# Paged attention over the cache in a hybrid decoder step: values read one slot later, sigmoids and buffers of the weight chain rearranged

## The chip, the cores and the metric

The kernel runs on one core of a Trainium2 chip, in float32. The metric is the device time of one execution in microseconds (us); lower is better. Below, PE is TensorE (matmuls), DVE is VectorE, ACT is ScalarE, POOL is GpSimd and SP is SyncE. Here POOL issues the gathers of cache pages and SP the other transfers.

## What is computed

A two-layer decoder step over 528 prompt positions and 64 sample positions (8 sequences of 8 tokens). Each layer is a feed-forward block, a mixer and a second feed-forward block. The mixer has an SSD part (a state-space scan) and a stick-breaking attention part with 8 heads of 64. The change touches the attention of the sample tokens to their past: 2048 cached positions per sequence, in 16 pages of 128.

```python
def sb_block(q, start, k, v, key_valid, bias):
    z = jnp.einsum('bqhd,bkhd->bhqk', q, k).astype(jnp.float32) * (SB_HEAD_DIM ** -0.5)
    z = z + bias.astype(jnp.float32)[None, :, None, None]
    ...
    log_stay = jnp.where(allowed, jax.nn.log_sigmoid(-z), 0.0)
    log_after = lax.cumsum(log_stay, axis=3, reverse=True) - log_stay
    w = jnp.where(allowed, jnp.exp(jax.nn.log_sigmoid(z) + log_after), 0.0)
    return jnp.einsum('bhqk,bkhd->bqhd', w.astype(v.dtype), v)
...
k_past = cache_k[l][page_table].reshape(db, -1, SB_HEADS, SB_HEAD_DIM)
v_past = cache_v[l][page_table].reshape(db, -1, SB_HEADS, SB_HEAD_DIM)
```

The weight of a key is its own sigmoid times the product of "what stays", sigmoid(-z), over all later keys. The kernel computes it with products instead of logarithms: a reverse running product of sigmoid(-z), shifted by one, times sigmoid(z).

## The kernel before

**Order.** The program is written in the order of `run`: feed-forward, mixer, feed-forward, for each layer. A list scheduler then sets the order of every engine's instructions before the run, by priorities and by its own timing; each engine works its list in order. Inside `mixer` the paged past (`past`) has the priority of its place in the program, and the other parts (convolution, scan, keys, gates, prompt attention, output projection) carry priorities of their own, so their matmuls stand between the slots of the past as filler.

**Slots.** `past` (L1458) works in slots x. In slot x the keys of sequence s = x // 4, part i = x % 4, are handled. Part i gathers two tiles of 128 x 1024 (`key_pages`, POOL, L1508), DVE transposes them in blocks into `kt` (`turned`, L1519), and PE multiplies 32 small matmuls into the PSUM bank `sc` (`scores`). There is one `sc` bank, and a new `sc` tile begins in every second slot. After every second slot ACT turns the bank into `be` = sigmoid(z) and `st` = sigmoid(-z), for two groups of four heads ("quads"): four ACTIVATEs of 128 x 256, in the order be, st, be, st (`sigmoids`, L1292 and L1293).

**The chain from scores to weights.** After a sequence's fourth slot `past_weights` (L1532) runs: DVE scans `st` of each quad (`stay`, L1298), takes the total product of each of four stretches (`tot`, L1537), PE transposes `tot`, DVE multiplies the carries of the later stretches into `car` (L1543 to L1545), PE transposes back, DVE copies `cq` (L1548). Then for each quad: DVE multiplies be x carry x shifted `st` (L1552) and the last column be x carry (L1553), PE transposes the result in four pieces into the one PSUM bank `pw` (L1556), and ACT copies it to the weight tile `wt` (L1558).

**Values.** In slot x the value pages of part vi = (x - 6) % 4 of sequence v = (x - 6) // 4 are also gathered (`value_pages`, L1569) and multiplied with the weights (`weigh`, 16 matmuls into `po`). So two slots lie between a sequence's last scores and its first values. The values of the last sequence follow after the loop. `gathered` collects `po` once per sequence (L1589 to L1594).

**What ties slots together.** `together` makes the first matmul of a slot wait for all that the slot's score and value matmuls read: `kt`, both value pages and both `wt`. Key and value pages share six buffers (tag `kn`). `be` and `st` share a pool of four (tag `pb`), one set, so a sequence's sigmoids take the buffers that the previous sequence's products and transposes free. `wt` has two buffers, one for each quad. `qbd`, the block-diagonal queries of a sequence, is one tile that ACT refills (L1471).

**After the past.** The four column pairs of the first half of the output projection stand behind `last_sc`, `last_pw` and `last_po`, the last score, weight and value matmuls.

Of the kernel before, what the change touches and what calls it, by code (L numbers as in the profile page):

```python
# [8 lines left out]
F32 = mybir.dt.float32  # L9
# [3 lines left out]
AF = mybir.ActivationFunctionType  # L13
ALU = mybir.AluOpType
# [13 lines left out]
def const_arrays():  # L28
    p = np.arange(128)
    f = np.float32  # L30
    a32 = np.arange(32)
    c = {}
    c["ident"] = np.eye(128)
    c["ones"] = np.ones((128, 1))
    c["half"] = p[:, None] // 64 == np.arange(32)[None, :]
    o8 = np.zeros((128, 64))
    q64 = np.arange(64)
    same = q64[:, None] // 8 == q64[None, :] // 8
    o8[:64] = same
    c["one8"] = o8  # L40
    c["srep"] = p[:, None] % 32 == p[None, :] % 32
    a16 = np.arange(16)[None, :]
    c["sel16"] = (p[:, None] % 8 == a16 % 8) & (p[:, None] // 32 % 2 == a16 // 8)
    c["mko"] = ((p[:, None] // 8) % 4 == np.arange(4)[None, :])
    sm = np.zeros((128, 8))
    sm[:64] = q64[:, None] // 8 == np.arange(8)[None, :]
    c["seqm"] = sm
    dsel = np.zeros((128, 8))
    for h in range(8):
        dsel[h, h] = 1.0  # L50
        dsel[32 + h, h] = 1.0
    c["dsel"] = dsel
    c["koff"] = ((p % 8) * 16)[:, None]
    c["voff"] = ((p % 32) * 4)[:, None]
    c["mg"] = p[:, None] // 8 == a16
    c["mx"] = p[:, None] // 32 == np.arange(4)[None, :]
    c["kt16"] = np.broadcast_to(np.arange(16)[None, :], (128, 16))
    return {k: np.ascontiguousarray(v.reshape(128, -1)).astype(f) for k, v in c.items()}
# [48 lines left out]
class Kern:  # L107
# [169 lines left out]
    def setup_rest(self):  # L277
        nc, I = self.nc, self.I
# [39 lines left out]
        for h in range(4):  # L318
            v = self.hp[32 * h:32 * h + 32, 32:48].rearrange("p (x h) -> p x h", h=4)[:, :, h]
# [4 lines left out]
        for m in range(4):  # L324
            v = self.hp[32 * m:32 * m + 32, 32:48].rearrange("p (l m h) -> p l m h", l=2, h=2)[:, :, m, :]
            o = self.bt4[32 * m:32 * m + 32, :].rearrange("p (s l h) -> p s l h", s=2, l=2)
# [24 lines left out]
        for l in range(2):  # L351
# [4 lines left out]
            vi = self.cst([128, 32, 2], f"vi{l}", I32)  # L356
# [11 lines left out]
        self.Cbd = [self.cst([128, 2, 128], f"cbd{i}") for i in range(1)]  # L368
        for t in self.Cbd:
            nc.gpsimd.memset(t, 0.0)  # L370
        self.car = [self.cst([128, 128], f"car{i}") for i in range(2)]
        self.tot = [self.cst([128, 128], f"tot{i}") for i in range(2)]
        for t in self.car + self.tot:
            nc.gpsimd.memset(t, 1.0)

        self.dtw = [self.cst([128, 4, 40], f"dtw{h}", F32R) for h in range(2)]
        for t in self.dtw:
            nc.gpsimd.memset(t.bitcast(F32), 0.0)
        self.zero = self.cst([128, 1], "zero")
        nc.gpsimd.memset(self.zero, 0.0)  # L380

# [1076 lines left out]
    def past(self):  # L1458


        nc, l = self.nc, self.l
        self.oP = self.cp.tile([128, 4, 64], F32, name="oP", tag="oP")
        wts = {}
        late = lambda x: (x // 4, x % 4)
        for x in range(34):
            s, i = late(x)
            v, vi = late(x - 6)
            if s < 8 and i == 0:
                qbd = self.QBD[0]
                for a in range(4):  # L1470
                    nc.scalar.copy(qbd[32 * a:32 * a + 32, :, a, :].rearrange("p (b m) q -> p b m q", b=4),  # L1471
                                   self.rep[32 * a:32 * a + 32, :, :, 8 * s:8 * s + 8])
                be = [self.kv.tile([128, 512], F32, name="pbe", tag="pb", bufs=4) for _ in range(2)]
                st = [self.kv.tile([128, 512], F32, name="pst", tag="pb", bufs=4) for _ in range(2)]
            if s < 8 and i % 2 == 0:
                sc = self.own("sc", [128, 2, 256])
            kns = self.key_pages(s, i) if s < 8 else None
            vs = self.value_pages(v, vi) if v >= 0 else None
            kts = self.turned(kns) if kns else None
            if v >= 0 and vi == 0:  # L1480
                po = self.own("po", [128, 512])
            with self.together():
                if kts:
                    self.scores(sc, i % 2, kts, qbd)
                if vs:
                    self.weigh(po, vi, vs, wts[v])
            if s < 8 and i % 2:
                for quad in range(2):
                    c = 2 * l + quad
                    f = lambda t: t.rearrange("p (i t) -> p i t", t=16)[:, :, 8 * (i // 2):8 * (i // 2) + 8]  # L1490
                    self.sigmoids(f(be[quad]), f(st[quad]), sc[:, quad].rearrange("p (t i) -> p i t", t=8),
                                  self.bq[:, c:c + 1], self.bq[:, 4 + c:5 + c])
            if v >= 0 and vi == 3:
                self.gathered(v, po)
            if s < 8 and i == 3:
                wts[s] = self.past_weights(s, be, st)
        po = self.own("po", [128, 512])
        for vi in range(4):
            vs = self.value_pages(7, vi)
            with self.together():  # L1500
                self.weigh(po, vi, vs, wts[7])
        self.gathered(7, po)
# [28 lines left out]

    def past_weights(self, s, be, st):  # L1532
        nc = self.nc
        tot, car = self.tot[s % 2], self.car[s % 2]
        for quad in range(2):
            self.stay(st[quad], 128, 0, 512)
            nc.vector.tensor_tensor(tot[:, quad:quad + 1], st[quad][:, 0:1], st[quad][:, 1:2], ALU.mult)  # L1537

        pt = self.own("pw", [128, 2, 128])
        nc.tensor.transpose(pt[:, 0], tot, self.ident)  # L1540
        tv = pt[0:2, 0].rearrange("s (h a q) -> s a h q", h=4, a=4)
        cv = car[0:2].rearrange("s (h a q) -> s a h q", h=4, a=4)
        nc.vector.tensor_copy(cv[:, 2], tv[:, 3])  # L1543
        nc.vector.tensor_tensor(cv[:, 1], tv[:, 2], cv[:, 2], ALU.mult)
        nc.vector.tensor_tensor(cv[:, 0], tv[:, 1], cv[:, 1], ALU.mult)  # L1545
        nc.tensor.transpose(pt[:, 1], car, self.ident)
        cq = self.small("cq", [128, 2])
        nc.vector.tensor_copy(cq, pt[:, 1, 0:2])  # L1548
        wts = []
        for quad in range(2):  # L1550
            c = cq[:, quad:quad + 1]
            nc.vector.scalar_tensor_tensor(be[quad][:, 0:511], be[quad][:, 0:511], c, st[quad][:, 1:512], ALU.mult, ALU.mult)  # L1552
            nc.vector.tensor_scalar(be[quad][:, 511:512], be[quad][:, 511:512], c, None, ALU.mult)  # L1553
            pw = self.own("pw", [128, 4, 128])
            for cc in range(4):
                self.last_pw = nc.tensor.transpose(pw[:, cc, :], be[quad][:, cc:512:4], self.ident).ins  # L1556
            wt = self.kv.tile([128, 4, 16, 8], F32, name="wt", tag="wt")
            nc.scalar.activation(wt.rearrange("p a x q -> p x a q"),  # L1558
                                 pw.rearrange("p c (h a q) -> p (c h) a q", h=4, a=4), AF.Copy)
            wts.append(wt)  # L1560
        return wts
# [61 lines left out]
def build(nc, inputs):  # L1623
    arrays, I, O = {}, {}, {}
    CA, CM = pack(const_arrays()), pack(mask_arrays())
    given = {k: np.ascontiguousarray(inputs[k]) for k in _INS}
    given["c_const"], given["c_mask"] = CA[1], CM[1]
    for name, a in given.items():
        arrays["in_" + name] = a
        I[name] = nc.dram_tensor("in_" + name, a.shape, mybir.dt.from_np(a.dtype), kind="ExternalInput").ap()  # L1630
    for name, shape in _OUTS:
        O[name] = nc.dram_tensor("out_" + name, shape, F32, kind="ExternalOutput").ap()
    with tile.TileContext(nc, schedule_with_timeline_sim=True) as tc:
        with ExitStack() as ctx:
            Kern(tc, ctx, I, O, CA, CM).run()
    return arrays
# [10 lines left out]
```

## Time and profile before

| | |
|---|---|
| median of 3 runs | 2681.26 us (2680.89 to 2694.74) |
| profiled execution, its own time | 2681.37 us |
| span in its trace | 2679.6 us |
| mean granted TensorE clock | 0.987 |
| mixer of layer 0 with the paged past | 521 to 846 us of the span |
| mixer of layer 1 with the paged past | 1848 to 2173 us |
| key gathers | 128 x 512 KB, 5.7 us median from issue to landing |

How to read the rows in the prediction. A timeline row is start, length (us), engine, line of the kernel, operation, output <- inputs, shapes, count, and in brackets the engine's idle time just before with what ended it. A group row ends with busy us, mean ns of one, and the idle time before. A waits row reads: who <- for whom: us in total, times, longest. The profile's names are the tiles' names: `pbe` and `pst` are `be` and `st` of the past.

### The profile page before, as it was taken

The numbers are of one execution on the slowest core, as the hardware profiler recorded it, in microseconds if no ns is written. First come the engines' busy times: TensorE is split into PE (matmuls) and PEld (weight loads), VectorE is DVE, ScalarE is ACT, GpSimd is POOL, SyncE is SP. The second block draws the span as 40 slices with busy tenths as digits, with TensorE's granted clock in tenths as the row PEclk, the third lists the DMA queues.
The fourth block names the chain that finished last, engine by engine and source line by source line (L and its number), as shares of the span: only waits on it lengthen the run. The fifth ranks groups of instructions, "written<-read, shape, count | busy, mean of one in ns | idle before, by whom it ended". The sixth has DMA issues, their size and how long they took to land.

```text
span 2679.6 us, 51326 instructions
## 1 busy us (share of the span) xinstructions
PE 2600.5 (97%) x21547; PEld 2466.6 (92%) x21547; DVE 1505.1 (56%) x3005; ACT 978.9 (37%) x1771; POOL 304.7 (11%) x288
## 2 busy tenths in 40 slices
PE   8999999999889999999999999999998899999999
PEld 7999999898657999999999999998886579999998
DVE  6434346397886743444554343465878957444444
ACT  3222224256564432222332222233566634223222
POOL 1000000034532100000000000001345411000000
PEclk9999999999989999999999999999998999999999
DMA  3232234467973222222222323244678731222222
GB/s 113 80 115 82 85 113 131 127 214 264 336 241 129 70 81 79 79 79 79 79 79 79 97 85 100 78 151 164 223 253 300 249 128 56 88 86 79 85 89 76
DMA packets 245112, 343.28 MB, mean 128 GB/s; under 512 B 32809, under 2 KB 196721, under 8 KB 244881
## 3 DMA queue, kind: packets, MB, share of 16 engines
q1 hardware_dynamic: 208016, 205.77, 24.7%
q0 software_dynamic: 36864, 134.23, 14.5%
q8 instruction: 169, 2.77, 0.4%
q14 instruction: 63, 0.51, 0.1%
HBM read 320.29 MB, written 19.66 MB: 127 GB/s over the span
## 4 chain that ended last, share of the span: by engine, by line
PE 84%; DVE 7%; issue 3%; ACT 3%; DMA 2%; POOL 1%; SPq 0%; DVEq 0%; POOLq 0%; ACTq 0%
PE g L605 72%; PE v L926 2%; DVE kt L1519 2%; PE po L211 1%; PE sc L211 1%; DMA v<-in_cache_v,vi 1%; DVE st L1298 1%; PE pw L476 1%; DMA kn<-in_cache_k,ki 1%; DVE pst L1298 1%; POOL v L1569 0%; PE z L208 0%; PE z L211 0%; DVE xl L447 0%; DVE wlo L596 0%
## 5 line engine op out<-in xcount | busy, mean ns | idle before, releaser
L605 PE MATMUL g<-xl,whi 128*128 128x296 f32 (+1 forms) x3392 | 1014.6, 299 | 2.7 <-DVE xl L447 2.7
L605 PE MATMUL g<-xh,wlo 128*128 128x296 f32 (+1 forms) x3392 | 1012.9, 299 | 2.0 <-DVE wlo L596 2.0
L605 PE MATMUL g<-xh,whi 128*128 128x296 f32 (+1 forms) x3392 | 1011.1, 299 | 1.5 <-DVE gs L231 1.2
L595 ACT ACTIVATE whi<-raw 128x512 fp32r<-128x512 f32 (+1 forms) x664 | 412.6, 622 | 1323.6 <-PE g L605 1240.5
L596 DVE TENSOR_TENSOR wlo<-raw,whi 128x512 fp32r<-128x512 f32 (+1 forms) x664 | 450.3, 678 | 582.8 <-ACT whi L595 529.7
L605 PEld LDWEIGHTS g<-xl,whi 128*128 128x128 f32 x3392 | 638.6, 188 | 5.6 <-DVE xl L447 3.6
L605 PEld LDWEIGHTS g<-xh,wlo 128*128 128x128 f32 x3392 | 638.7, 188 | 4.3 <-DVE wlo L596 2.5
L605 PEld LDWEIGHTS g<-xh,whi 128*128 128x128 f32 x3392 | 638.7, 188 | 4.0 <-DVE gs L231 1.4
L605 PE MATMUL g<-hl,whi 128*128 128x296 f32 (+1 forms) x1408 | 417.8, 297 | 0.0
L605 PE MATMUL g<-hh,wlo 128*128 128x296 f32 (+1 forms) x1408 | 417.6, 298 | 0.0
L605 PE MATMUL g<-hh,whi 128*128 128x296 f32 (+1 forms) x1408 | 416.7, 298 | 0.0
L1508 POOL DMA_INDIRECT kn<-in_cache_k,ki x128 | 128.3, 1003 | 1657.9 <-PE g L605 934.8
L605 PEld LDWEIGHTS g<-hl,whi 128*128 128x128 f32 x1408 | 265.2, 188 | 0.0
L605 PEld LDWEIGHTS g<-hh,wlo 128*128 128x128 f32 x1408 | 264.3, 188 | 0.0
L605 PEld LDWEIGHTS g<-hh,whi 128*128 128x128 f32 x1408 | 263.9, 188 | 0.0
L1519 DVE STREAM_TRANSPOSE kt<-kn 128x512 f32<-128x512 f32 x256 | 162.9, 681 | 27.7 <-PE sc L211 14.5
L704 DVE SCALAR_TENSOR_TENSOR x<-g,x 128x296 f32<-128x296 f32 (+1 forms) x192 | 88.1, 463 | 119.1 <-PE g L605 118.5
L1569 POOL DMA_INDIRECT v<-in_cache_v,vi x128 | 143.3, 1119 | 100.0 <-DVE kt L1519 36.1
L231 DVE TENSOR_TENSOR us<-g,R 128x296 f32<-128x296 f32 (+1 forms) x176 | 81.5, 464 | 129.1 <-PE g L605 129.0
L231 DVE TENSOR_TENSOR gs<-g,R 128x296 f32<-128x296 f32 (+1 forms) x176 | 80.6, 463 | 126.2 <-PE g L605 121.3
L691 ACT ACTIVATE hh<-us 128x592 fp32r<-128x592 f32 (+1 forms) x88 | 61.2, 696 | 64.3 <-DVE us L689 64.3
L605 PE MATMUL g<-mh,whi 128*128 128x296 f32 (+1 forms) x256 | 77.7, 312 | 2.4 <-ACT mh L1277 1.3
(372 smaller groups left out, 2838.8 us busy)
## 6 DMA issues: line engine op xcount, KB each, us to landing
raw<-in_ffn_w_gu SPq DMA_DIRECT2D x176, 512.0 KB
raw<-in_ffn_w_down SPq DMA_DIRECT2D x80, 512.0 KB
raw<-in_w_in SPq DMA_DIRECT2D x44, 512.0 KB
raw<-in_w_out SPq DMA_DIRECT2D x16, 512.0 KB
spill<-x SPq DMA_DIRECT2D x16, 296.0 KB
x<-spill SPq DMA_DIRECT2D x16, 296.0 KB
raw<-in_ffn_w_down SPq DMA_DIRECT2D x16, 256.0 KB
xt<-in_x_prompt SPq DMA_DIRECT2D x8, 256.0 KB
```

The source lines that it names most:

```text
L211: i = self.nc.tensor.matmul(*a, **k).ins
L231: self.nc.vector.tensor_tensor(tv[0:P, h, :], ps[h][0:P, 0:self.n], rv[0:P, h, :], ALU.mult)
L595: nc.scalar.activation(hi[:, 0:nk], s, AF.Copy)
L596: nc.vector.tensor_tensor(lo[:, 0:nk], s, hi[:, 0:nk].bitcast(F32), ALU.subtract)
L605: mm = nc.tensor.matmul(ps[h][:, 0:self.n], w[:, k, :], self.hv(x)[:, h, :], start=(first and k == 0 and i == 0), stop=(last and k == nk - ...
L691: nc.scalar.activation(hh[:, a:b], u[:, a:b], AF.Copy)
L704: nc.vector.scalar_tensor_tensor(v, p, 0.5, v, ALU.mult, ALU.add)
L926: nc.tensor.matmul(ps[c], x[:, t0:t0 + 128], w.rearrange("p x c -> p (x c)"), start=(k == 0 and i == 0), stop=(k == 7 and i == 2))
L1298: self.nc.vector.tensor_tensor_scan(sv, sv, self.zero[0:rows].to_broadcast([rows, b - a - 1]), 1.0, ALU.mult, ALU.add)
L1508: self.nc.gpsimd.indirect_dma_start(kn, None, self.kflat, bass.IndirectOffsetOnAxis(ap=self.kidx[self.l][:, s, 2 * i + u:2 * i + u + 1], a ...
L1519: self.nc.vector.transpose(kt[:, 2 * u:2 * u + 2].rearrange("p t h i -> p t (h i)"), kns[u][:, :, 256 * quad:256 * quad + 256])
L1569: self.nc.gpsimd.indirect_dma_start(v.rearrange("p k c -> p (k c)"), None, self.vflat, bass.IndirectOffsetOnAxis(ap=self.vidx[self.l][:, s ...
```

## The change

Seven edits. Values follow one slot later: v = (x - 7) // 4, so three slots lie between a sequence's last scores and its first values, and the loop has 35 slots. `wt` gets a third buffer. `st` becomes two fixed tiles `self.pst` of 513 columns whose last column is a constant 1, and the pool `pb` keeps two buffers, for `be` alone. With that column the product L1552 covers all 512 columns, and the one-column product L1553 is dropped. The sigmoids come as st, st, be, be. `tot` and `car` become single tiles. An unused constant (`srep`) goes.

```diff
-        self.car = [self.cst([128, 128], f"car{i}") for i in range(2)]
-        self.tot = [self.cst([128, 128], f"tot{i}") for i in range(2)]
-        for t in self.car + self.tot:
+        self.car, self.tot = self.cst([128, 128], "car"), self.cst([128, 128], "tot")
+        for t in (self.car, self.tot):
             nc.gpsimd.memset(t, 1.0)
...
+        self.pst = [self.cst([128, 513], f"pst{i}") for i in range(2)]
+        for t in self.pst:
+            nc.gpsimd.memset(t[:, 512:513], 1.0)
...
-        for x in range(34):
+        for x in range(35):
             s, i = late(x)
-            v, vi = late(x - 6)
+            v, vi = late(x - 7)
...
-                be = [self.kv.tile([128, 512], F32, name="pbe", tag="pb", bufs=4) for _ in range(2)]
-                st = [self.kv.tile([128, 512], F32, name="pst", tag="pb", bufs=4) for _ in range(2)]
+                be = [self.kv.tile([128, 512], F32, name="pbe", tag="pb", bufs=2) for _ in range(2)]
+                st = self.pst
...
-                for quad in range(2):
-                    c = 2 * l + quad
-                    f = lambda t: t.rearrange("p (i t) -> p i t", t=16)[:, :, 8 * (i // 2):8 * (i // 2) + 8]
-                    self.sigmoids(f(be[quad]), f(st[quad]), sc[:, quad].rearrange("p (t i) -> p i t", t=8),
-                                  self.bq[:, c:c + 1], self.bq[:, 4 + c:5 + c])
+                for out, scale, c0 in ((st, -0.125, 4), (be, 0.125, 0)):
+                    for quad in range(2):
+                        c = c0 + 2 * l + quad
+                        o = out[quad][:, 0:512].rearrange("p (i t) -> p i t", t=16)[:, :, 8 * (i // 2):8 * (i // 2) + 8]
+                        nc.scalar.activation(o, sc[:, quad].rearrange("p (t i) -> p i t", t=8), AF.Sigmoid,
+                                             scale=scale, bias=self.bq[:, c:c + 1])
...
-        tot, car = self.tot[s % 2], self.car[s % 2]
+        tot, car = self.tot, self.car
...
-            nc.vector.scalar_tensor_tensor(be[quad][:, 0:511], be[quad][:, 0:511], c, st[quad][:, 1:512], ALU.mult, ALU.mult)
-            nc.vector.tensor_scalar(be[quad][:, 511:512], be[quad][:, 511:512], c, None, ALU.mult)
+            nc.vector.scalar_tensor_tensor(be[quad], be[quad], c, st[quad][:, 1:513], ALU.mult, ALU.mult)
...
-            wt = self.kv.tile([128, 4, 16, 8], F32, name="wt", tag="wt")
+            wt = self.kv.tile([128, 4, 16, 8], F32, name="wt", tag="wt", bufs=3)
```

ACT's list in layer 0, where the weights of sequence 3 are copied (`wt`) and the first half of sequence 4 goes through the sigmoids; `zsg` is a gate's sigmoid, `whi` a weight split, `cbd` a copy for the scan. Before:

```order
L1248 ACT_TABLE_LOAD
L1248 ACTIVATE zsg<-zi 128x592
L1292 ACTIVATE pbe<-sc,bq 128x32x8
L1293 ACTIVATE pst<-sc,bq 128x32x8
L1116 COPY cbd_1948<-xc 64x128 x2
L1558 ACTIVATE wt<-pw 128x16x4x8
L1292 ACTIVATE pbe<-sc,bq 128x32x8
L595 ACTIVATE whi<-raw 128x512
L1558 ACTIVATE wt<-pw 128x16x4x8
L1293 ACTIVATE pst<-sc,bq 128x32x8
L1086 ACT_TABLE_LOAD
```

The same place in the changed kernel, where L1493 is the line of all four sigmoids:

```order
L596 ACTIVATE whi<-raw 128x512
L1493 ACT_TABLE_LOAD
L1493 ACTIVATE pst_1958<-sc,bq 128x32x8
L1493 ACTIVATE pst_1959<-sc,bq 128x32x8
L1559 ACTIVATE wt<-pw 128x16x4x8
L1493 ACTIVATE pbe<-sc,bq 128x32x8
L1117 COPY cbd_1948<-xc 64x128 x2
L1493 ACTIVATE pbe<-sc,bq 128x32x8
L596 ACTIVATE whi<-raw 128x512
L1249 ACTIVATE zsg<-zi 128x592
L880 ACTIVATE hsq<-k 128x592 x4
L1559 ACTIVATE wt<-pw 128x16x4x8
```

The last of the four sigmoids now stands ahead of the second `wt` copy instead of behind it. Over the whole program the list holds 74 ACT_TABLE_LOAD rows where it held 58, eight more in each layer.

PE's list in layer 0 at slot 6; `g` are matmuls of the projections. Before:

```order
L605 MATMUL g_7561<-xh,whi 128x296
L605 MATMUL g_7561<-xl,whi 128x296
L208 MATMUL sc<-kt,qbd_1946 32x128
L211 MATMUL sc<-kt,qbd_1946 32x128 x15
L211 MATMUL po<-v,wt 32x256 x8
L996 MATMUL cop<-call,co 27x128
```

In the changed kernel the same slot has scores alone, at the same row of the list:

```order
L606 MATMUL g_7529<-xh,whi 128x296
L606 MATMUL g_7529<-xl,whi 128x296
L207 MATMUL sc<-kt,qbd_1946 32x128
L210 MATMUL sc<-kt,qbd_1946 32x128 x15
L997 MATMUL cop<-call,co 27x128
L606 MATMUL g_7530<-xh,whi 128x296
```

The first value matmuls moved to slot 7, with some 49 filler matmuls between the two slots.

DVE's list at the end of the chain of sequence 0; `cacc` and `u` belong to the convolution. Before:

```order
L981 SCALAR_TENSOR_TENSOR cacc<-u,par,cacc 128x616
L1552 SCALAR_TENSOR_TENSOR pbe<-pbe,cq,pst 128x511
L1553 TENSOR_SCALAR pbe<-pbe,cq 128x1
L1552 SCALAR_TENSOR_TENSOR pbe<-pbe,cq,pst 128x511
L1553 TENSOR_SCALAR pbe<-pbe,cq 128x1
```

In the changed kernel:

```order
L982 SCALAR_TENSOR_TENSOR cacc<-u,par,cacc 128x616
L1554 SCALAR_TENSOR_TENSOR pbe<-pbe,cq,pst_1958 128x512
L1554 SCALAR_TENSOR_TENSOR pbe<-pbe,cq,pst_1959 128x512
L982 SCALAR_TENSOR_TENSOR cacc<-u,par,cacc 128x616
L971 TENSOR_TENSOR u<-g_7359,R 128x296
```

The two one-column products are gone, and the two products follow each other.

More of the change, by code (lines that the diff above doesn't have):

```diff
@@ L40, in const_arrays @@
     c["one8"] = o8
-    c["srep"] = p[:, None] % 32 == p[None, :] % 32
     a16 = np.arange(16)[None, :]
```

## The prediction

> **What bounds the kernel now.** I read the page first, then the busy times by stretch, then PE's waits in the two stretches that matter, then the order of time around one sequence.
>
> ```profile
> span 2679.6 us, 51326 instructions
> PE 2600.5 (97%) x21547; PEld 2466.6 (92%) x21547; DVE 1505.1 (56%) x3005; ACT 978.9 (37%) x1771; POOL 304.7 (11%) x288
> ```
>
> The kernel is TensorE-bound as a whole: PE is idle for 2679.6 - 2600.5 = 79.1 us. A change outside the matmuls can win only that idle time, and time in which the clock was held back. The stretches (columns: length, busy us of PE, PEld, DVE, ACT, POOL, clock, DMA share, GB/s) say where both lie:
>
> ```profile
> 521.00:846.00 325.00, 296.83 (x3408) 241.49 (x3410) 270.90 (x627) 190.20 (x400) 126.51 (x120) 0.96 0.74 253
> 846.00:1848.00 1002.00, 1000.17 (x7329) 992.36 (x7322) 473.83 (x848) 297.75 (x482) 17.81 (x14) 1.00 0.28 86
> 1848.00:2173.00 325.00, 295.67 (x3378) 239.13 (x3377) 270.31 (x617) 188.11 (x394) 129.54 (x120) 0.95 0.74 253
> ```
>
> The first and third rows are the two mixers, from the first score matmul to the end of the paged past. There PE is idle 28.2 + 29.3 = 57.5 us, and the clock of 0.96 and 0.95 costs 0.04 x 325 + 0.05 x 325 = 29 us. Between them lie 1000 us with PE full. So the change plays inside some 87 us, and only where the past causes the loss.
>
> Here is what ends PE's idle time, layer 0 and then layer 1 (waits in total, times, longest):
>
> ```profile
> PE sc L208 <- DMA v<-in_cache_v,vi: 4.8, 6, 1.6
> ...
> PE pw L1556 <- ACT wt L1558: 3.1, 2, 1.6
> PE pw L1540 <- DVE tot L1537: 2.2, 1, 2.2
> ...
> PE po L208 <- ACT wt L1558: 1.0, 1, 1.0
> ```
> ```profile
> PE sc L208 <- ACT qbd L1471: 6.0, 2, 3.3
> PE zt L1350 <- ACT wt L1558: 2.6, 1, 2.6
> PE pw L1540 <- DVE tot L1537: 2.5, 1, 2.5
> ...
> PE pw L1556 <- DVE pbe L1553: 1.1, 2, 0.7
> PE pw L1556 <- ACT wt L1558: 0.9, 1, 0.9
> ```
>
> Leaving the DMA row aside, these are steps of the chain that the change edits: 6.3 us in layer 0, 13.1 us in layer 1, 19.4 us together. The other 38 us belong to prompt attention, the scan and transfers.
>
> Why the chain sets the pace is seen in slots 16 to 18 of layer 0 (PE, start us and length; slot 18 is the first to use the weights of sequence 3):
>
> ```profile
> 667.10 0.27 PE L208 MATMUL sc<-kt,qbd 128*32 128x128 f32 x1 [0.72 <-DMA v<-in_cache_v,vi]
> ...
> 675.08 0.27 PE L208 MATMUL sc<-kt,qbd 128*32 128x128 f32 x1 [0.46 <-DMA v<-in_cache_v,vi]
> ...
> 678.09 0.63 PE L1556 MATMUL pw<-call,pbe 128*128 128x128 f32 x4
> 681.98 0.63 PE L1556 MATMUL pw<-call,pbe 128*128 128x128 f32 x4
> ...
> 686.39 0.30 PE L208 MATMUL sc<-kt,qbd 128*32 128x128 f32 x1
> ```
> ```profile
> 781.78 0.30 PE L208 MATMUL sc<-kt,qbd 128*32 128x128 f32 x1
> ...
> 805.73 0.30 PE L208 MATMUL sc<-kt,qbd 128*32 128x128 f32 x1
> ```
>
> Slots 16 and 17 are 8.0 us apart; slot 18 comes 11.3 us after slot 17, and 4.4 us after the last weight transposes. For a later sequence (slots 29 and 30) the same step takes 23.9 us. Every fourth step waits for the chain. ACT shows the second reason:
>
> ```profile
> 676.85 0.47 ACT L1292 ACTIVATE pbe<-sc,bq 128x256 f32<-128x256 f32 x1 [0.71 <-DVE pbe L1553]
> 677.61 0.47 ACT L1293 ACTIVATE pst<-sc,bq 128x256 f32<-128x256 f32 x1 [0.28 <-DVE pbe L1552]
> ...
> 682.65 0.60 ACT L1558 ACTIVATE wt<-pw 128x512 f32<-128x512 f32 x1 [0.92 <-PE pw L1556]
> 683.14 0.47 ACT L1293 ACTIVATE pst<-sc,bq 128x256 f32<-128x256 f32 x1
> ```
>
> The sigmoids of the next sequence need the buffers that the old one frees: two at the DVE products, two at the transposes. The last sigmoid comes after the last transposes, and the scores of slot 18 need the one `sc` bank that it empties. So slot 18 waits for weights **and** for sigmoids. The change lifts the first wait; the second stays, with a shorter chain ahead of it.
>
> **The change part by part.** The durations of the instructions it touches:
>
> ```profile
> L1553 DVE TENSOR_SCALAR pbe<-pbe,cq 128x1 f32<-128x1 f32 x32 | 6.5, 203 | 0.0
> L1298 DVE TENSOR_TENSOR_SCAN pst<-pst,zero 128x511 f32<-128x511 f32 x32 | 37.6, 1197 | 0.8 <-ACT pst L1293 0.8
> L1292 ACT ACT_TABLE_LOAD x19 | 24.4, 1283 | 14.8 <-DVE pbe L1552 11.4 <-PE sc L211 3.2
> ```
>
> *A, the chain.* How closely sigmoids follow each other:
>
> ```profile
> 627.74 0.47 ACT L1292 ACTIVATE pbe<-sc,bq 128x256 f32<-128x256 f32 x1
> 628.11 0.47 ACT L1293 ACTIVATE pst<-sc,bq 128x256 f32<-128x256 f32 x1
> ```
>
> They start 0.37 us apart. The scan of quad 0 needs its `pst` sigmoid, which stood second and now stands first, so it starts 0.37 us earlier; the scan of quad 1 follows it on DVE (1.20 us each) and ends 0.37 us earlier too. The two removed one-column products take 2 x 0.20 = 0.4 us out. After the last transposes one sigmoid (0.47 us) now stands where a weight copy and a sigmoid stood (682.65 to 683.61, 0.96 us): 0.5 us. That is 1.3 us for each sequence; seven pacing steps a layer make the past of both layers 18 us shorter. The order says more: between the first scan and the second product of each sequence DVE has 283 + 307 instructions before and 277 + 274 after, 16 of the 39 fewer being the removed ones. What reaches the end is only PE idle that goes, 19.4 us at most and 0 at least. The third `wt` buffer and the extra slot should end the waits that name `wt` (3.1 + 1.0 + 2.6 + 0.9 = 7.6 us), the shorter DVE part some of the rest: I take half, **-10 us**.
>
> *B, the clock.* It drops where PE stalls:
>
> ```profile
> 730.00:740.00 10.00, 8.57 (x126) 5.35 (x115) 10.00 (x22) 4.15 (x8) 7.19 (x6) 1.00 0.93 325
> 740.00:750.00 10.00, 7.73 (x48) 5.63 (x47) 10.00 (x23) 5.46 (x13) 3.31 (x3) 0.70 0.87 300
> ```
> ```profile
> 743.33 0.66 PE L1350 MATMUL zt<-call,be 128*128 128x128 f32 x4 [2.08 <-DVE be L1343]
> ```
>
> In proportion, 10 of 57.5 us of idle take 29 x 10 / 57.5 = 5 us of lost clock with them; ends 0 and -10 (for all 19.4). I take **-5 us**. The Trainium skill (TensorE: Matmul & The Clock Gate, HAM oscillation) states that only idle gaps over about 3.4 us throttle; by that this term is 0 and the sum 2675 us. The trace differs here: the longest gap in the 0.70 row is 2.08 us.
>
> *C, the DVE products.* 32 x 0.203 = 6.5 us of DVE go. Outside the chain they lie under 271 of 325 us of DVE work that PE rarely waits for: **-1 us**, ends 0 and -6.5. Widening the product by a column is inside the 738 ns of its group.
>
> *D, table loads.* The order has 74 table loads where it had 58, eight more in each layer, because the new sigmoid order falls apart around the scan's exponentials: 16 x 1.283 = 20.5 us of ACT. They hide where ACT idles (190 of 325 us busy); ends 0 and +20.5. PE's waits on past weights and `qbd`, all on ACT, are 13.6 us against 378 us of ACT work, under 0.04 us a us, which would give 0.7; but these loads stand inside the chain, so I take **+4 us**. If ACT had no idle cover, all 20.5 would show.
>
> ```profile
> 611.22 0.60 ACT L1558 ACTIVATE wt<-pw 128x512 f32<-128x512 f32 x1
> 611.84 1.28 ACT L1292 ACT_TABLE_LOAD   x1
> 613.13 0.47 ACT L1292 ACTIVATE pbe<-sc,bq 128x256 f32<-128x256 f32 x1
> ```
>
> The Trainium skill (ScalarE: Activation LUTs, What ACT_TABLE_LOAD costs) adds about 1.38 us of drain to each load, 2.66 us a switch, which would make 42.6 us of D. The trace agrees on the load itself and shows no drain: 0.02 us before and 0.01 us after.
>
> *E, one slot later.* Values begin a slot later and three value-only slots instead of two follow the last scores. PE has as many matmuls as before, so 0; at most one group of 16 (1.05 us, row below) stands bare in each layer: **+1 us**, ends 0 and 2.1.
>
> ```profile
> 806.63 1.05 PE L211 MATMUL po<-v,wt 128*32 128x256 f32 x16
> ```
>
> The gathers keep their number and the six shared buffers, and on POOL's queue the value pair still follows the key pair. Single `tot` and `car` tiles add waits on transposes a sequence back, 30 to 40 us old: 0. The fixed `pst` tiles free when the pooled ones did: 0.
>
> Sum: -10 - 5 - 1 + 4 + 1 = -11 us on the profiled execution's 2681.37 us (0.11 us above the median shown): **2670 us**.
>
> **The rivals.**
> - *The pace stays.* Slot 18's scores still need the bank that the last sigmoid empties, so every fourth step keeps its length and only the waits on `wt` go: -7.6 + 4 = -4, 2678 us. For it: 683.61 lies after 682.65, the sigmoid is the later of the two. Against: fewer DVE instructions lie in the chain.
> - *The whole chain loss goes.* A and B at their ends, the rest as above: -19.4 - 10 - 1 + 4 + 1 = -25, 2656 us. For it: the order of layer 1, the worse one before, now has 33 fewer DVE instructions in its chains.
> - *Slower: the table loads enter the pacing loop.* Where ACT alternates between the scan's exponentials and the halves of the sigmoids, each extra load delays the copy or sigmoid the next slot waits for, and no idle of ACT covers it. It decides from the point where the eight loads, 10.3 us a layer, outweigh the 9 us a layer that A takes out of the chain; with A gone and D and E full: +20.5 + 2 = +22, 2704 us, halfway +11, 2692 us. Against: ACT is idle 42% of the stretch.
>
> **How the numbers follow.** The forecast has 0.38, the unchanged pace 0.25, the whole loss 0.22, the slower case 0.15. Within 0.5% (13.4 us, about what a measurement of this kernel can tell from no change) of 2681.3 lie the unchanged pace, most of the forecast and the small end of the slower case; below 2668 the whole loss and two fifths of the forecast: faster 0.37, same 0.50, slower 0.13. The unknown costs reach from -36 (A, B, C full, D and E 0) to +22 us; leaving out a tenth on each side the range is 2648 to 2690 us.
>
> **What would show it.** After: no TENSOR_SCALAR on `pbe`; PE's waits naming `wt` near 0 and those naming `tot` and `qbd` smaller; PE idle in the two mixer stretches nearer 47 than 57 us and clocks above 0.96; steps into slots 18 and 30 shorter than 11.3 and 23.9 us; 74 table loads, ACT busy 20 us higher. The prediction is wrong if those steps keep their length, if PE waits name ACT more than before, or if the mixers gain what the wait for key and value pages then takes back.

## The result, and the profile after

The changed kernel takes 2706.28 us (median of 4 runs, 2700.43 to 2707.57) against 2683.73 us (4 runs). The ratio is 1.0064, with a 95% interval of 1.0043 to 1.0086: 0.6% slower, where 0.4% faster was forecast. The profiled execution takes 2707.47 us, its span is 2705.3 us, and its mean granted clock is 0.979 where it was 0.987.

The page after:

```profile
span 2705.3 us, 51292 instructions
PE 2616.3 (97%) x21547; PEld 2478.8 (92%) x21547; DVE 1500.7 (55%) x2973; ACT 998.6 (37%) x1787; POOL 303.9 (11%) x288
```

PE has the same 21547 matmuls. It is idle for 2705.3 - 2616.3 = 89.0 us (79.1 before), and busy 15.8 us longer. The clock explains the longer work: (1 - clock) x span is 34.8 us before and 56.8 us after. So of the 26 us by which the span grew, idle time has 10 and the clock, by this count, up to 22. The two overlap, since the count takes in time in which PE was idle at half clock.

The busy times by stretch (length, busy us of PE, PEld, DVE, ACT, POOL, clock, DMA share, GB/s), with both mixers from the first score matmul to the output projection:

```profile
523.00:860.00 337.00, 304.03 (x3399) 245.65 (x3399) 267.35 (x603) 200.20 (x407) 125.85 (x120) 0.93 0.72 245
860.00:1872.00 1012.00, 1009.83 (x7332) 1000.50 (x7331) 476.14 (x856) 298.07 (x483) 18.43 (x14) 0.99 0.28 85
1872.00:2210.00 338.00, 301.34 (x3417) 244.56 (x3417) 268.62 (x609) 200.04 (x407) 129.51 (x120) 0.93 0.72 245
```

Each mixer takes 12 to 13 us more than the 325 us of before. PE is idle for 33.0 + 36.7 us in them (28.2 + 29.3), and the clock is 0.93 in both (0.96 and 0.95).

What ends PE's idle time now, layer 0 and then layer 1:

```profile
PE sc L207 <- DMA v<-in_cache_v,vi: 7.0, 6, 3.3
PE po L207 <- DMA v<-in_cache_v,vi: 3.7, 3, 1.8
...
PE z L1324 <- ACT st L1341: 2.6, 2, 1.4
...
PE po L210 <- DVE oP L1595: 2.2, 2, 1.2
...
PE sc L207 <- ACT pbe L1493: 1.5, 1, 1.5
...
PE pw L1557 <- ACT wt L1559: 1.3, 2, 0.7
```
```profile
PE sc L207 <- DMA v<-in_cache_v,vi: 8.3, 5, 3.7
PE po L210 <- DVE oP L1595: 4.8, 3, 2.4
...
PE po L207 <- ACT wt L1559: 1.5, 1, 1.5
```

The waits on `tot` and `qbd` are gone and those on `wt` are small. The DMA row has grown, and the result copy `oP` (L1595) is new.

The paced steps in layer 0, slots 17 to 19 and 29 to 31 (start of each slot's first score matmul):

```profile
681.49 0.27 PE L207 MATMUL sc<-kt,qbd 128*32 128x128 f32 x1 [1.43 <-DMA v<-in_cache_v,vi]
...
690.40 0.27 PE L207 MATMUL sc<-kt,qbd 128*32 128x128 f32 x1 [0.40 <-DMA v<-in_cache_v,vi]
...
699.42 0.30 PE L207 MATMUL sc<-kt,qbd 128*32 128x128 f32 x1
...
793.79 0.42 PE L207 MATMUL sc<-kt,qbd 128*32 128x128 f32 x1
...
806.44 0.30 PE L207 MATMUL sc<-kt,qbd 128*32 128x128 f32 x1 [1.53 <-ACT pbe L1493]
...
811.92 0.30 PE L207 MATMUL sc<-kt,qbd 128*32 128x128 f32 x1
```

The step into slot 18 takes 8.9 us (11.3 before), the step into slot 30 12.7 us (24.0). Yet the past is no shorter: layer 0 from the first score to the end of the last value matmul takes 314.8 us (315.9), layer 1 326.4 us (319.1). What the paced steps gave up, their neighbours took: summed over layer 0 from slot 10 on, the steps into slots 4s+6 fell from 96.2 to 76.2 us, and those into 4s+7, 4s+8 and 4s+9 rose by 6.5, 5.6 and 8.6 us. Behind the past, from the last value matmul to the output projection, layer 0 takes 22.0 us (9.2 before) and layer 1 11.1 us (5.9): in layer 0 all of the 12 us lie there, in layer 1 some 5 of them.

One place shows how the clock enters. Behind the past of layer 0 some prompt attention is left over and runs alone. PE's timeline there:

```profile
839.21 0.23 PE L1324 MATMUL z<-mall 128*128 128x128 bf16 x1
...
841.29 0.22 PE L1324 MATMUL z<-mall 128*128 128x128 bf16 x1 [1.44 <-ACT st L1341]
...
843.11 1.11 PE L1351 MATMUL zt<-call,be 128*128 128x128 f32 x4 [0.90 <-ACT st L1341]
...
850.04 0.47 PE L207 MATMUL zo<-wp,vk 128*64 128x128 f32 x1 [0.53 <-ACT wp L1353]
```

and the stretches of the same place:

```profile
838.50:842.00 3.50, 2.06 (x18) 1.25 (x14) 1.58 (x4) 2.69 (x6) 0.00 (x0) 0.99 0.00 0
842.00:858.00 16.00, 13.39 (x73) 10.61 (x72) 10.78 (x27) 10.61 (x22) 0.00 (x0) 0.50 0.13 50
```

A gap of 1.44 us is followed by 16 us at half the clock, though PE is busy for 13.4 of them: by (1 - clock) x length 8 us lost, of which PE was idle for part. The four transposes at 843.11 take 1.11 us where 128 x 128 transposes at full clock took 0.63. Before, behind the gap of 2.08 us at 743.33, the same can be read:

```profile
742.00:744.00 2.00, 0.67 (x7) 0.68 (x7) 2.00 (x5) 1.40 (x4) 1.70 (x2) 0.99 0.98 350
744.00:754.00 10.00, 9.81 (x53) 7.93 (x53) 9.00 (x22) 5.96 (x13) 0.08 (x1) 0.50 0.59 184
```

### The profile page after: what moved, and what is told of

It reads as the page before. It is cut to its first block, busy times and chain, and to the rows that moved or that the text cites. A ratio compares the mean times of both kernels' runs of the same rounds, so it can differ in the third digit from the quotient of the medians.

```text
span 2705.3 us, 51292 instructions
## 1 busy us (share of the span) xinstructions
PE 2616.3 (97%) x21547; PEld 2478.8 (92%) x21547; DVE 1500.7 (55%) x2973; ACT 998.6 (37%) x1787; POOL 303.9 (11%) x288
## 4 chain that ended last, share of the span: by engine, by line
PE 85%; DVE 5%; ACT 5%; DMA 3%; issue 2%; SPq 0%; POOL 0%; DVEq 0%; POOLq 0%; ACTq 0%
PE g L606 73%; PE v L927 2%; DMA v<-in_cache_v,vi 2%; DVE kt L1521 1%; PE po L210 1%; PE sc L210 1%; ACT L1112 1%; ACT dec L1112 1%; PE pw L477 1%; ACT L1493 1%; DVE st L1299 1%; PE po L207 0%; PE z L210 0%; PE z L207 0%; DVE xl L448 0%
## 5 line engine op out<-in xcount | busy, mean ns | idle before, releaser
L210 PE MATMUL po<-v,wt 128*32 128x256 f32 x996 | 72.8, 409 | 7.0 <-DVE oP L1595 7.0
```

Source lines behind the costliest of these rows:

```text
L210: i = self.nc.tensor.matmul(*a, **k).ins
```

## The experiments

Ratios are to the kernel before on the same chip. "Clock" is the mean over all runs of that kernel. "Idle" and "lost" are span minus PE busy, and (1 - clock) x span, of its profiled run; with a clock of three digits "lost" is good to some 1.4 us. The kernel before had a mean clock of 0.983 to 0.984 on the four other chips and a median of 2688 to 2712 us there.

| kernel | values behind by | ratio (95%) | clock | idle, us | lost, us |
|---|---|---|---|---|---|
| changed kernel | 3 slots | 1.0064 (1.0043 to 1.0086) | 0.981 | 89.0 | 56.8 |
| late_only | 3 | 1.0057 (1.0037 to 1.0078) | 0.979 | 100.7 | 51.6 |
| chain_only | 2 | 1.0012 (0.9992 to 1.0032) | 0.983 | 96.4 | 48.9 |
| old_sig | 3 | 1.0079 (1.0056 to 1.0103) | 0.979 | 103.4 | 57.4 |
| sig_only | 2 | 1.0017 (0.9996 to 1.0037) | 0.982 | 89.6 | 46.1 |
| share_ctl | 3 | 1.0051 (1.0033 to 1.0070) | 0.978 | 99.0 | 57.2 |
| wt4 | 3 | 1.0031 (1.0012 to 1.0050) | 0.983 | 84.5 | 48.5 |
| lag6_wt4 | 2 | 1.0017 (0.9996 to 1.0038) | 0.983 | 85.5 | 48.5 |
| lag8 | 4 | 1.0179 (1.0154 to 1.0205) | 0.974 | 99.4 | 65.5 |
| split_after | 3 | 1.0097 (1.0067 to 1.0128) | 0.978 | 87.7 | 54.2 |
| lag6_kn7 | 2 | 1.0054 (1.0037 to 1.0070) | 0.979 | 91.5 | 51.7 |
| lag7_kn7 | 3 | 1.0125 (1.0108 to 1.0143) | 0.976 | 108.8 | 71.6 |
| base_kn7 | 2 | 1.0033 (1.0018 to 1.0048) | 0.981 | 90.3 | 37.9 |
| before_x15 | 2 | 1.0065 (1.0043 to 1.0088) | 0.978 | 96.0 | 60.0 |
| after_x15 | 3 | 1.0061 (1.0040 to 1.0081) | 0.980 | 104.4 | 54.6 |
| before_sc300 | 2 | 1.0023 (1.0008 to 1.0039) | 0.982 | 89.0 | 51.6 |
| after_sc300 | 3 | 1.0099 (1.0070 to 1.0129) | 0.977 | 99.2 | 62.9 |
| warm_after | 3 | 1.0075 (1.0050 to 1.0100) | 0.980 | 95.2 | 60.1 |
| warm_lag6 | 2 | 0.9982 (0.9965 to 1.0000) | 0.988 | 91.9 | 27.0 |

### One part at a time

`late_only` is the kernel before with the later values (and the third `wt` buffer and single `tot` and `car` that they need):

```diff
-        for x in range(34):
+        for x in range(35):
-            v, vi = late(x - 6)
+            v, vi = late(x - 7)
-            wt = self.kv.tile([128, 4, 16, 8], F32, name="wt", tag="wt")
+            wt = self.kv.tile([128, 4, 16, 8], F32, name="wt", tag="wt", bufs=3)
```

> Values one slot later alone: three wt buffers and single tot and car tiles (their memory pays for the third wt), sigmoids and products as before. Its list has 72 table loads (before 58, the change 74), and behind the last value matmuls of layer 0 it leaves 4 zt matmuls and no scores z of prompt attention, as before does (the change leaves 12 zt and 13 z). If the leftover prompt attention is the cause: 2684 us, within 6 of before. If the table loads are: 2700 to 2706. If values coming later are the cause, through the six buffers of the gathers: 2700 to 2706.

`chain_only` is the changed kernel with these three lines put back, so the new chain without lateness:

> The other half alone: fixed pst tiles, the product over 512 columns, sigmoids st, st, be, be, but values two slots behind and two wt buffers as before. Its list has 60 table loads, and in layer 0 it leaves 12 z, 12 zt and 20 zo matmuls of prompt attention behind the last value matmuls. If the leftover prompt attention is the cause: 2695 to 2706 us. If the table loads are: 2680 to 2687. If values coming later are: 2680 to 2687.

`old_sig` is the changed kernel with the sigmoids in the old order:

```diff
-                for out, scale, c0 in ((st, -0.125, 4), (be, 0.125, 0)):
-                    for quad in range(2):
+                for quad in range(2):
+                    for out, scale, c0 in ((be, 0.125, 0), (st, -0.125, 4)):
```

> The change with the sigmoids in the old order be, st, be, st. Its list has 60 table loads and leaves 4 zt and no z of prompt attention behind the past in layer 0. If the leftover prompt attention is the cause: 2680 to 2687 us. If the table loads are: 2680 to 2687. If values coming later are: 2700 to 2706.

`sig_only` is the kernel before with its four sigmoids in the new order, st, st, be, be, and nothing else:

> The kernel before with the sigmoids in the order st, st, be, be and nothing else. Its list has 56 table loads and leaves 8 zt and no z behind the past in layer 0. If the leftover prompt attention is the cause: 2684 to 2692 us. If the table loads or the later values are: 2680 to 2685.

The two kernels with later values cost 0.6% and 0.8%; the two without, 0.1% and 0.2%, can't be told from no change. Table loads are not the cause: `old_sig` lists 60 of them (58 before, 74 after) and is no faster than `late_only` with 72 or the change with 74. Prompt attention left over behind the past of layer 0 is not the general cause either: in `late_only` and `old_sig` only four zt transposes and 22 zo matmuls stand there, as before the change (12 and 24 in the changed kernel).

### Why later values cost: weight buffers, lag, gating

`share_ctl` makes room by letting three pairs of small tiles share a buffer (one of them below); every engine's list is that of the changed kernel.

```diff
-        self.tn = self.small("tn", [128, 4, 64], bufs=1)
+        self.tn = self.sm.tile([128, 4, 64], F32, name="tn", tag="qs", bufs=1)
```

> The changed kernel with the three pairs of small tiles sharing a buffer, still with three weight buffers; every engine's list is that of the changed kernel. Control for the runs with a fourth weight buffer. All theories: ratio 1.005 to 1.008. If it is 1.003, the fourth weight buffer did nothing and theory W has no support.

`wt4` adds a fourth weight buffer to it (`bufs=4` in place of `bufs=3`), so that no copy of new weights waits for the last reader of the old:

> The changed kernel with a fourth buffer for the weight tiles, so that both quads' copies for the next sequence can be made while the old weights are still read. Room for it comes from three pairs of small tiles that now share a buffer (cs and bt, co and hs, qs and tn). Theory W (with values three slots behind, the wait for the weight copy lies between slots 4s+6 and 4s+7, one slot behind the wait for the sigmoids' bank, where before both lay on the same step): the separate wait goes, ratio to the kernel before at most 1.002, steps into slots 4s+7 back near 7 us. Theory D (every further slot of lateness adds a slot with keys alone and one with values alone, and these cost more than the full slot that goes): nothing changes, ratio near 1.006.

`lag6_wt4` and `lag8` are the same with `late(x - 6)` in 34 slots and `late(x - 8)` in 36:

> The same kernel (four weight buffers, shared small tiles, the new chain with fixed tiles) with values two slots behind, as before the change. Theory W: the wait for the weight copy goes from step 4s+6, the bank's wait stays there: ratio 0.998 to 1.002. Theory D: lateness is back to that of before, ratio 0.999 to 1.003. It gives the base for the other two lags.

> The same kernel with four weight buffers and values four slots behind, in 36 slots. Theory D: lateness costs by the slot, so two slots later than before cost twice what one does: ratio near 1.012. Theory W: with four buffers no weight copy lies between two slots at this distance, ratio 1.000 to 1.003.

`split_after` is the changed kernel with the group of a slot's matmuls cut in two:

```diff
-            with self.together():
-                if kts:
+            if kts:
+                with self.together():
                     self.scores(sc, i % 2, kts, qbd)
-                if vs:
+            if vs:
+                with self.together():
                     self.weigh(po, vi, vs, wts[v])
```

> The changed kernel with the score matmuls and the value matmuls of a slot in two groups, so that the first score matmul no longer waits for value pages and weights. Theory W: slot 4s+7's scores do not wait for the weight copy any more, ratio at most 1.002. Theory G (the scores are held by the value pages, whose gathers queue behind the key pages in the six shared buffers): also at most 1.002, and the waits of sc on v go from PE's list, with po on v in their place. Theory D: ratio stays near 1.006.

The fourth buffer gives 1.0031 against 1.0051 of its control. The intervals overlap, so a gain is possible but not shown, and the value lies between W's 1.002 and D's 1.006. `lag8` speaks against W and beyond D: 1.8% for two extra slots where D had 1.2%, and the steps from lag to lag (0.0014, then 0.0148) are far from equal. `split_after` is no faster than the changed kernel, at 1.0097: the scores no longer wait for pages, but PE's waits of `po` on v come to 25 us in both mixers (3.9 in the changed kernel). Gating by the group is not what costs.

The named waits are no safe guide here: `share_ctl`, with the very list of the changed kernel on another chip, took 329.8 us for the past of layer 0 (314.8), and had 6.8 us of `sc` waiting on v where the changed kernel had 15.3, and 27.7 us of waits in scan and convolution where that had 14.4 (sums of the idle times in PE's timeline over both mixers).

Even a shorter past is not yet a gain. In `lag6_wt4` that of layer 0 took 302.8 us, 13 less than in the kernel before, but 22.5 us of other work stood behind it where 9.2 had: from the first score to the output projection 325.3 us, against 325.1.

### A seventh page buffer

```diff
-            kn = self.kv.tile([128, 1024], F32, name="kn", tag="kn", bufs=6)
+            kn = self.kv.tile([128, 1024], F32, name="kn", tag="kn", bufs=7)
```

In the new chain without lateness, in the changed kernel (there paid for with one temporary tile of six), and in the kernel before:

> The new chain with fixed tiles, values two slots behind, two weight buffers, and a seventh page buffer (7 where 6 were), paid for by the shared small tiles. Theory G (the page gathers through the six shared buffers set the pace once the chain's stall is gone): ratio 0.993 to 0.999, PE waits on v under 3 us for both layers. Theory O (what a list loses lies in many small gaps that differ from list to list, and the clock adds as much again): ratio 0.998 to 1.005 with the waits on v smaller and others in their place.

> The changed kernel (values three slots behind, three weight buffers) with a seventh page buffer, paid for by the shared small tiles and by five temporary tiles where six were. Theory G: ratio at most 1.002, PE waits naming v well under the 19 us of the changed kernel. Theory W (the weight copy between slots 4s+6 and 4s+7): stays at 1.005 to 1.007. Theory O: anywhere from 1.001 to 1.008, with waits on v smaller and others in their place.

> The kernel before with a seventh page buffer alone (room from the shared small tiles, single tot and car tiles, no srep). Theory G: the chain's stall still hides the gathers, so little comes of it: 0.997 to 1.001. Theory O: 0.998 to 1.005.

All three are slower, by 0.54%, 1.25% and 0.33%. In `lag6_kn7` the waits of `sc` on v fell to 2.7 us in both mixers (8.3 in `chain_only`), but PE's waits in the chain rose from 4.3 to 9.2 us and those of `sc` on anything else from 11.0 to 21.6 (the same sums), and no clock was won. Theory G falls. More room made each kernel slower than its version without, which pointed away from resources and to the order of the list; no run holds the list fixed while a buffer is added.

### The order of the filler alone

The scheduler takes the rest of the mixer by priority numbers (UNIT). `before_x15` multiplies all of them by 1.5 in the kernel before; `before_sc300` adds 300 to the four numbers of the scan:

```diff
-    "scan0": 467, "scan2": 75,
-    "scan3": 879, "scan5": 123,
+    "scan0": 767, "scan2": 375,
+    "scan3": 1179, "scan5": 423,
```

`after_x15` and `after_sc300` do the same to the changed kernel.

> The kernel before with all priority numbers of the filler units (UNIT) times 1.5: nothing of the past, its buffers or its lag changes, but about 1700 rows of PE's list move. Theory L (values later cost by themselves): ratio 0.998 to 1.002. Theory O (the order of the filler sets the size of the loss): 1.003 to 1.010, with PE idle and lost clock up together.

> The changed kernel with the same numbers times 1.5; no prompt attention is left behind the past. Theory L: 1.004 to 1.008, as without it. Theory O: can be anywhere from 0.998 to 1.012, and not farther from before_x15 than the two shifts are from each other.

> The kernel before with 300 added to the four priority numbers of the scan's units. Theory L: 0.998 to 1.002. Theory O: 1.003 to 1.010.

> The changed kernel with 300 added to the same four numbers. Theory L: 1.004 to 1.008. Theory O: anywhere from 0.998 to 1.012. If both changed kernels lie as far above their own twin as the change does above the kernel before (0.6%), lateness costs by itself, whatever the order.

In the kernel before, whose past, lag and buffers are untouched, another order costs 0.65% and 0.23%: the first is as much as the whole change, the second lies between what L and O had forecast. The changed kernel stands 0.04% below its twin in one order and 0.76% above it in the other, 0.64% above in the original one. So theory L in its plain form falls, lateness has no fixed price; but O in its plain form, that the change is only a reshuffle, isn't shown either, since two of three pairs have lateness at 0.6 to 0.8%. The page of `before_x15` shows the same signature as the change:

```profile
span 2726.3 us, 51315 instructions
PE 2630.3 (96%) x21547; PEld 2485.0 (91%) x21547; DVE 1505.3 (55%) x3005; ACT 986.7 (36%) x1777; POOL 311.3 (11%) x288
```

96.0 us idle and, at a clock of 0.978, 60.0 us lost.

### Filling a gap

In the table the ratio goes with the clock, but that may be cause or company. Two kernels give PE something to do in a gap: transposes of the identity that nothing reads, 24 in each layer.

```diff
+        if i >= 11:
+            for _ in range(8):
+                nc.tensor.transpose(z[0][:, 0:128], self.ident, self.ident)
...
                 p = new("zt")
+                if i >= 10:
+                    for _ in range(4):
+                        nc.tensor.transpose(p[:, 0:128], self.ident, self.ident)
```

> The changed kernel with extra transposes of the identity that nothing reads: eight in the z bank of prompt unit 11, four in each zt bank of units 10 and 11, 24 in each layer, 3.8 us of PE work at 0.158 us each, put where PE waits for sigmoids and scans behind the past of layer 0. Theory C (the gap brings the half clock, and the half clock is most of its price): the half clock of 18 us behind the past of layer 0 (8.5 us lost in the changed kernel, 5.1 in its control) is gone or at most one quantum of 1.7 us, the stretch from the last value matmul to the output projection falls from 22 and 19 us to 14 to 17, and the ratio to the kernel before falls to 1.002 to 1.004. Theory N (the clock goes down for other reasons): the half clock stays, the stretch is as long or longer by up to 3.8 us, ratio 1.005 to 1.008.

> The kernel of lag6_wt4 (new chain, values two slots behind, four weight buffers) with the same 24 extra transposes a layer. Without them 8.5 us were lost to the half clock behind the past of layer 0, from 832.7 on. Theory C: that goes but for at most 1.7 us, ratio 0.998 to 1.000, which would be as fast as the kernel before or faster. Theory N: 1.001 to 1.004.

The stretch behind the past of layer 0 in `lag6_wt4` (without):

```profile
832.00:834.00 2.00, 0.92 (x6) 0.37 (x6) 1.97 (x4) 2.00 (x6) 0.00 (x0) 0.81 0.00 0
834.00:850.00 16.00, 14.28 (x75) 11.03 (x76) 9.67 (x26) 9.98 (x20) 0.00 (x0) 0.50 0.14 54
```

and in `warm_lag6` (with):

```profile
840.00:843.00 3.00, 1.59 (x12) 1.05 (x12) 2.93 (x6) 3.00 (x9) 0.00 (x0) 1.00 0.00 0
843.00:859.00 16.00, 13.79 (x134) 11.92 (x132) 10.07 (x28) 10.61 (x22) 0.00 (x0) 1.00 0.22 77
```

The gap that was 1.40 us is 0.49, and the half clock doesn't come. The first row is of `lag6_wt4`, the others are of `warm_lag6`:

```profile
832.10 0.22 PE L1324 MATMUL z<-mall 128*128 128x128 bf16 x1 [1.40 <-ACT st L1341]
```
```profile
838.81 1.07 PE L1326 MATMUL z<-call 128*128 128x128 f32 x8
...
840.43 0.22 PE L1327 MATMUL z<-mall 128*128 128x128 bf16 x1 [0.49 <-ACT st L1344]
...
842.25 0.66 PE L1355 MATMUL zt<-call 128*128 128x128 f32 x4 [0.98 <-ACT st L1344]
...
845.64 0.32 PE L207 MATMUL zo<-wp,vk 128*64 128x128 f32 x1 [1.32 <-ACT wp L1359]
```

But gaps of 0.98 and 1.32 us follow, and PE is no busier than where the half clock came: 1.94 of the 3.41 us from 839.29 to 842.70, against 1.97 of the 3.41 us ahead of the dip in the changed kernel (838.48 to 841.89). So the half clock stayed away, but that the shorter gap kept it away is not shown.

From the last value matmul to the output projection layer 0 takes 18 us where it took 23, with 48 matmuls more in the program. The ratio falls from 1.0017 to 0.9982, on two chips, each against the kernel before on its own. That is 9 us, and it is the only one of the table's 19 kernels below 1, at the edge of what can be told from no change. A rival stays open: the added matmuls also moved other work in the lists (64 of ACT's 1773 instructions stand elsewhere than in `lag6_wt4`, against some 150 in `before_sc300`), and behind the past of layer 1 stand 38 zo matmuls where 24 were. How much of the 9 us is the gap and how much the order is not separated. `warm_after` shows half of it: the 8.5 us lost behind layer 0 (5.1 in its control) became 3.4 in two dips, but that stretch takes 23 us, no less than without (22, and 19 in the control), and its ratio of 1.0075 can't be told from the 1.0064 and 1.0051 without. There theory C was half right on the clock (it had at most 1.7 us) and wrong on the time.

## Why the prediction was wrong

**Where the loss lies: right.** The play is in the two mixers. Their idle time and lost clock, 57.5 and 29 us in the prediction's rows, are 69.7 us and, by 0.07 x 337 + 0.07 x 338, 47 us after: 30 us more, where the span grew by 26.

**A, the chain, -10: the waits went, the time didn't.** Waits that name steps of the chain fell from 19.4 us to the 4.3 us quoted above and 2.3 us in rows not quoted (`wt` ahead of `sc`, `pbe` in layer 1), 12.8 us less; the steps into 4s+6 fell by 20 us in layer 0, twice the 9 forecast. The step that failed is the sentence from there to the end: "seven pacing steps a layer make the past of both layers 18 us shorter". Those steps did not pace the past, because PE hardly waited in them: its list has filler matmuls there. The step of 11.3 us into slot 18, which the prediction shows as a wait, is PE work from end to end (11.31 of 11.31 us):

```profile
675.08:686.39 11.31, 11.31 (x123) 9.77 (x123) 11.24 (x26) 6.29 (x12) 4.66 (x5) 1.00 1.00 354
```

From slot 10 on the steps into 4s+6 take 193 us in both layers before the change, and PE is idle for 18 of them; after it, 161 us and 12. So 32 us of step gave 6 us of idle time, and the rest was work that had to be done elsewhere. The past took 314.8 and 326.4 us where it had taken 315.9 and 319.1. The slots around the steps took the work, and waits for value pages rose from 10.2 to 19.2 us, those around the results' gathering (`ob`, `oP`) from 1.3 to 7.9. Two signs that the prediction had named for being wrong came: that one, and PE's waits that name ACT, which rose from 26.3 to 30.8 us over both mixers. `chain_only`, the chain alone, stands at 1.0012 (0.9992 to 1.0032), so no gain shows from this part even without lateness.

**B, the clock, -5: wrong sign, and the largest error.** It was tied in proportion to idle time that would go. Measured: up to +22 us of lost clock on 10 us more idle time, with PE busy 15.8 us longer. Proportion is the wrong model: a gap of 1.44 us was followed by 16 us at half clock in the changed kernel, and gaps of 0.49, 0.98 and 1.32 us by none in `warm_lag6`. The test named for it, clocks above 0.96, failed at 0.93. The Trainium skill (TensorE: Matmul & The Clock Gate, HAM oscillation) gives the rule that no idle gap should exceed some 3.4 us. Read as the prediction read it, that only such gaps throttle, it fails on the same rows: the gap was 1.44 us.

**C, the DVE products, -1: right as far as it can be seen.** No one-column product is left and DVE is busy 4.4 us less; `chain_only` shows no gain from it.

**D, table loads, +4: the work came, its price didn't.** ACT is busy 19.7 us more, as worked out (20.5), but `old_sig` with 60 loads is no faster than the changed kernel with 74 (1.0079 and 1.0064). The slower rival, table loads in the pacing loop, gave 2692 to 2704 us, near the 2707.5 measured, for a reason that this run speaks against: that its number came close is luck.

**E, one slot later, +1: mis-sized.** This edit was priced by what it adds to PE, nothing, plus a bare group of matmuls. `late_only` puts it at 0.57%, some 15 us, clock and idle time included. The price depends on the order of the rest of the mixer: under two other orders the whole change cost 0.0% and 0.8%. That it comes out of the new order which the later values force on the filler fits these runs, but is argued, not shown: no run moved the values and kept the order. Which feature of an order makes its gaps is not settled. The weight copy, the page buffers and the grouping of scores with values were each tried and are not enough to explain it.

The rival "the pace stays" (2678 us) was right that the past keeps its length, but not why: it had every fourth step keep its own, and these fell by 20 us in layer 0. Its number failed with E and B.

## What to carry to other kernels

A longer step is a wait only as far as its engine is idle in it, and a shorter one is no gain until the stage around it is shorter: read the length from the first matmul of the stage to where the filler behind it is done too, and not the step or the wait that was aimed at. Where a list scheduler places filler, run the unchanged kernel in another order first: here that alone was worth 0.2 to 0.65%, so a single edit's 0.6% says little about the edit. Count an idle gap of TensorE with the clock behind it: 1.44 us of idle time stood ahead of 16 us at half clock here. Matmuls that nothing reads may be the cheaper filling where a gap's place is sure, but of two kernels with them one gained, by 0.35% and not apart from its new order, and one did not.

## What the hardware did that was not expected

The granted clock took two values, full and 0.50, but for stretches in which it changes. In windows of 0.85 us over both mixers and the 100 us behind each, the loss comes in steps of 1.7 us, 3.4 us at half clock each: 14 dips with 34 us lost in all before the change, 16 dips with 51 us after, single ones of up to 8.5 us. All of a run's dips start whole multiples of 3.413 us apart, as on a grid that the program's work doesn't move. A dip can start after 1.4 us of idle time and can last while PE is busy for 9.81 of 10 us. The Trainium skill (TensorE: Matmul & The Clock Gate, The HAM clock gate) gives a window of about 3.4 us and a clock that is either full or half; both agree with these rows, but that it takes a whole idle window to throttle does not.

Idle time as the profile shows it doesn't settle when a dip comes. In the changed kernel one starts at 1377.8 us, in the 1000 us between the mixers, behind 3.41 us in which the profile shows PE busy throughout:

```profile
1374.38:1377.79 3.41, 3.41 (x31) 3.41 (x30) 1.24 (x7) 0.00 (x0) 0.00 (x0) 1.00 0.49 153
1377.79:1381.20 3.41, 3.41 (x16) 3.41 (x16) 1.97 (x10) 0.64 (x1) 0.00 (x0) 0.50 0.00 1
```

What the clock goes by is not found here.

One kernel's time also follows its clock from run to run: in 30 runs of the kernel before on one chip, between 2699 and 2723 us and clocks between 0.978 and 0.989, 0.010 less clock went with 18 us more. Differences of half a per cent need many runs on one chip.
